# First attention pass on half the array: paired high products for the later query blocks, decay added by VectorE

## Chip, cores and metric

One NeuronCore of a Trainium2 chip runs the whole program as one launch. The metric is the device time of one execution in microseconds (us), as the median of several runs. A smaller number is better.

## What is computed

The reference is one layer of a streaming encoder over 2048 positions of width 1024: a normalisation, one combined projection whose columns are split between eight gated-mixing heads (A) and eight attention heads (B), an output projection, a feed-forward part with a short causal convolution, and a last normalisation, all in float32. The change touches the attention heads alone:

```
def forgetting_attention(q, k, v, f_logit):
    ...
    c = jnp.cumsum(jax.nn.log_sigmoid(f_logit.astype(jnp.float32)), axis=1)
    ...
        s = jnp.einsum('bhtd,bshd->bhts', qi, k, preferred_element_type=jnp.float32) * scale
        s = s + ci[..., :, None] - c[:, :, None, :]
        ...
        s = jnp.where(kpos[None, :] <= qpos[:, None], s, -jnp.inf)
        p = jax.nn.softmax(s, axis=-1)
        return jnp.einsum('bhts,bshd->bthd', p.astype(v.dtype), v)
```

Every score gets a decay, `c[t] - c[s]`, where `c` is a running sum per head. A number that is the same for all keys of one query drops out in the softmax.

## The kernel before

**Precision by parts.** TensorE's operands are kept as a rounded high part and the low remainder. A product of two matrices is then three matmuls (high by high, high by low, low by high), which add up in one PSUM bank. `mm3` does this for the projections: lines 207, 209 and 211, each with 128 rows of contraction and 512 moving columns.

**Stages.** Stage A projects the input (`a_half`). Stage C is the output projection (`c_half`). Stage D is the first half of the feed-forward part (`d_half`, `d_up`). After them come the second half of the tokens and the down projection. The attention is a generator, `b_stream`, that runs as a fill beside these stages: after every projection matmul `tick` counts, and after every 3.5 to 4.4 ticks (`RATES`) it takes one step of the generator. The pieces come in the order query block 0 to 3 (`tb`, 512 queries each) and in it head 0 to 7.

**A piece of attention.** `b_max` is the first pass over a head and a query block: for every key block `sb` of 512 keys up to the diagonal and every chunk `tt` of 128 queries it makes the scores, their least value (scores carry the opposite sign) and a sum of exponentials. `b_mix` is the second pass, which makes the scores again the other way round (lines 774 and 775), exponentiates, and multiplies by the values (lines 762 and 763).

**A chunk of the first pass.** The queries lie in DRAM as `qx` (rows 0 to 63 high, 64 to 127 low), the keys as `kx` (rows 0 to 63 low, 64 to 127 high, 128 and 129 ones, 130 and 131 the decay of the keys in two parts). `cc` holds the decay of the queries. Line 713 multiplies tile `t1` (high queries, `cc`, ones) by tile `m1` (high keys, ones, key decay), so that the decay comes out of the same matmul as the high product: 96 rows of contraction. Line 714 multiplies `t2` by `m2`, both with 128 rows, which gives the two mixed products. Both lines write one PSUM tile of 512 columns, which is called `s` or `dn`: `scores` hands out three tiles `s` and, from stage D on (`self.more`), two tiles `dn` in turn. Off the diagonal VectorE reduces it to its minimum (line 717); on the diagonal it adds the mask and reduces in one instruction (line 719). ScalarE then exponentiates in place (line 722), which frees the tile.

**Decay.** `a_forget` runs four times, once per block of 512 tokens. It transposes a small tile of 16 rows (line 565), makes the running sum `c` (lines 592 to 595), splits it into two parts and writes them to `cc` and to `kx` (lines 597 to 603).

**What sets the order.** The code emits instructions with priorities (the fill and the weight preparation run ahead of their place), and a scheduler with a model of the machine then lays down one fixed order for every engine; on the chip each engine works through its own list in that order. All loads and most stores stand in SyncE's queue (line 99); GpSimd issues the stores of lines 895 and 937 and rounds the weights (line 149). PE in the profile is TensorE, PEld its loading of stationary operands, DVE is VectorE, ACT ScalarE, POOL GpSimd and SP SyncE.

Of the kernel before, what the change touches and what calls it, by code (L numbers as in the profile page):

```python
# [18 lines left out]
P = 128  # L19
# [6 lines left out]
TB = 512  # L26
# [12 lines left out]
BUFS = {  # L39
    "raw": 2, "rawl": 3, "whi": 5, "wlo": 5, "thi": 2, "tlo": 2, "acc": 4,  # L40
# [11 lines left out]
def f32(ap):  # L52
    return ap.bitcast(F32)
# [26 lines left out]
class Block:  # L80
# [134 lines left out]
    def constants(self):  # L215
        nc, a, tc = self.nc, self.a, self.tc
        cp = self.cpool = self.ctx.enter_context(tc.tile_pool(name="const", bufs=1))
        self.ident = cp.tile([P, P], F32, name="ident")
        make_identity(nc, self.ident)
        self.mhalf = cp.tile([P, 8], F32, name="mhalf")  # L220
        nc.gpsimd.memset(self.mhalf, -0.5)
        self.colA = cp.tile([P, 112], F32, name="colA")
        self.colB = cp.tile([P, 88], F32, name="colB")
        self.halo = cp.tile([P, 2 * NF, 2], F32, name="halo")
        nc.gpsimd.memset(self.halo, 0.0)
        dp = self.ctx.enter_context(tc.tile_pool(name="dram", bufs=1, space=DRAM))
        self.ones_d = dp.tile([2, HALF], F32, name="ones_d")
        t = lambda n, k, s: [dp.tile(s, F32, name=f"{n}{i}") for i in range(k)]
        self.qx = t("qx", 2, [8, 128, HALF])
        self.kx = t("kx", 2, [8, 132, HALF])  # L230
        self.cc = t("cc", 2, [8, 2, HALF])
        self.vd = t("vd", 2, [HALF, 8, P])
        self.mixh = t("mixh", 4, [D, TB])
        self.mixl = t("mixl", 4, [D, TB])
        self.rows_d = [t(f"rows{i}_", 8, [P, D]) for i in range(2)]
        self.act_d = [t(f"act{i}_", NF, [P, HALF]) for i in range(2)]
        self.tw_d = t("tw", NF // 2, [P, 2, D])
# [311 lines left out]
    def a_forget(self, half, b):  # L549

        nc, sp, pp = self.nc, self.sp, self.ap
        hT = self.hT[b]
        pl = self.til(pp, [16, TB], F32, "mm")
        for k in range(KC):
            nc.tensor.matmul(pl, lhsT=self.wf[:, k, :], rhs=hT[0][:, k, :], start=k == 0, stop=False)
            self.tick()
            nc.tensor.matmul(pl, lhsT=self.wf[:, k, :], rhs=hT[1][:, k, :], start=False, stop=k == KC - 1)
            self.tick()
        lg = self.til(sp, [16, TB], F32, "ln")
        nc.scalar.activation(lg, pl, AF.Copy)  # L560

        def turn():
            pt = self.til(pp, [P, 4, 16], F32, "tp")
            for i in range(4):
                nc.tensor.transpose(pt[:, i, :], lg[:, i * P:(i + 1) * P], self.ident[:16, :16])
# [12 lines left out]
            nc.vector.tensor_tensor(d, d, ru, op=ALU.mult)  # L578
            nc.scalar.activation(lu, u, AF.Ln)
            nc.vector.tensor_tensor(lu, lu, d, op=ALU.subtract)  # L580
            nc.vector.scalar_tensor_tensor(lu, z, 0.0, lu, op0=ALU.min, op1=ALU.subtract)
            lh = self.til(sp, [P, 4, 8], F32R, "fr")
            ll = self.til(sp, [P, 4, 8], F32R, "fr")
            nc.vector.tensor_copy(lh, lu)
            nc.vector.tensor_tensor(ll, lu, f32(lh), op=ALU.subtract)
            self.defer(70, lambda: cumulate(lh, ll))

        def cumulate(lh, ll):
            pc = self.til(pp, [8, TB], F32, "tp")
            for i in range(4):  # L590
                w, o = self.tri[:, 0:TB - P * i], pc[:, P * i:]
                nc.tensor.matmul(o, lhsT=lh[:, i, :], rhs=w, start=i == 0, stop=False)
                nc.tensor.matmul(o, lhsT=ll[:, i, :], rhs=w, start=False, stop=i == 3)
            c = self.til(sp, [8, TB], F32, "ln")
            nc.vector.tensor_scalar(c, pc, self.carry, None, ALU.add)
            nc.vector.tensor_copy(self.carry, c[:, TB - 1:TB])
            for sc, dst in ((-1.0, self.cc[half]), (1.0, self.kx[half][:, 130:132, :])):
                hl = self.til(sp, [8, 2, TB], F32R, "vn")
                rh, rl = hl[:, 0, :], hl[:, 1, :]
                nc.scalar.activation(rh, c, AF.Copy, scale=sc)  # L600
                nc.vector.scalar_tensor_tensor(rl, c, sc, f32(rh), op0=ALU.mult, op1=ALU.subtract)
# [78 lines left out]
    def b_keys(self, h, sb, values):  # L680
# [9 lines left out]
        self.dma(f32(v), self.vd[hf][sl, h, :].rearrange("(c p) d -> p c d", p=P))  # L690
        return m1, m2, v

    def b_max(self, h, tb):

        nc, bp, pp = self.nc, self.bp, self.bpp
        hf, sl = tb // 2, slice((tb % 2) * TB, (tb % 2 + 1) * TB)
        self.T1.append(self.T1.pop(0))
        t1 = self.T1[0]
        t2 = self.til(self.mp, [P, TB], F32R, "t2")
        self.dma(f32(t1[0:64, :]), self.qx[hf][h, 0:64, sl])  # L700
        self.dma(f32(t1[64:66, :]), self.cc[hf][h, :, sl])
        self.dma(f32(t2), self.qx[hf][h, :, sl])
        nm = self.til(bp, [P, 4, 4], F32, "part")
        ls = self.til(bp, [P, 4, 4], F32, "ls")
        if h % 2 == 0:
            self.rr = self.til(bp, [P, 4, 2], F32, "rr")
        for sb in range(tb + 1):
            m1, m2 = self.b_keys(h, sb, False)
            for tt in range(4):
                ts = slice(tt * P, (tt + 1) * P)  # L710
                n = TB if sb < tb else (tt + 1) * P
                ps = self.scores([P, TB])
                nc.tensor.matmul(ps[:, :n], lhsT=t1[0:96, ts], rhs=m1[0:96, :n], start=True, stop=False)  # L713
                nc.tensor.matmul(ps[:, :n], lhsT=t2[:, ts], rhs=m2[:, :n], start=False, stop=True)  # L714
                dst = nm[:, tt, sb:sb + 1]
                if sb < tb:
                    nc.vector.tensor_reduce(dst, ps, axis=AX.X, op=ALU.min)  # L717
                else:
                    nc.vector.tensor_tensor_reduce(ps[:, :n], ps[:, :n], self.mask[:, 384 - tt * P:], 1.0, 3.0e38,
                                                   ALU.add, ALU.min, dst)  # L720

                nc.scalar.activation(ps[:, :n], ps[:, :n], AF.Exp, scale=-1.0, bias=dst, accum_out=ls[:, tt, sb:sb + 1])  # L722
                yield
        mx = self.til(bp, [P, 4], F32, "mx")
        if tb:
# [3 lines left out]
        m8 = self.til(bp, [P, 4, 2], F32R, "m8")  # L729
# [3 lines left out]
        if tb:  # L733
            k = slice(0, tb + 1)
# [732 lines left out]
```

## Time and profile before

| | |
|---|---|
| median of three runs | 2483.25 us (2481.99 to 2483.38) |
| the profiled execution's own time | 2483.0 us |
| its span, first to last instruction | 2481.3 us |
| mean granted TensorE clock | 0.995 of full speed |
| busy: PE, DVE, ACT, POOL | 98%, 70%, 55%, 14% of the span |

The page gives busy time per engine, the span in 40 slices, the DMA queues, the chain of work that ended last, and the costliest groups of instructions. A group's row reads: line, engine, operation, tile written <- tiles read, shapes, count | busy us, mean ns of one | idle us of the engine before them and what ended most of it. In the timeline a row is: start, duration, engine, line, operation. A matmul's duration there holds its way through the array, and the next one starts before it ends, so what a matmul costs is the step from one start to the next. Shapes are partitions x columns; `16*128` means that 16 rows are contracted and the stationary operand has 128 columns.

### The profile page before, as it was taken

Reading aid. Unit: us, or ns where it says so; the run is one execution under the profiler, and the core shown is the slowest. Engines: PE = TensorE matmul, PEld = TensorE weight load, DVE = VectorE, ACT = ScalarE, POOL = GpSimd, SP = SyncE. Lnnn points to the kernel's source line nnn. Section 1 sums busy time; section 2 is a strip of 40 time slices with the busy share of each in tenths; the row PEclk is TensorE's granted clock in tenths of the full one; section 3 lists DMA queues with packets and bytes.
Section 4 is the critical chain, followed back from the end, with each engine's and each line's share of the span. In section 5 each row is a group of like instructions: output and inputs, shape, how many; then the busy total and the mean of one; then the engine's idle time right before and its main releaser. Section 6 shows DMA issues by size and latency. Waiting matters only on the chain.

```text
span 2481.3 us, 33045 instructions
## 1 busy us (share of the span) xinstructions
PE 2430.5 (98%) x11082; PEld 1995.2 (80%) x11082; DVE 1742.9 (70%) x3116; ACT 1367.4 (55%) x2651; POOL 335.6 (14%) x343
## 2 busy tenths in 40 slices
PE   7998999999999999999999999999999999999998
PEld 5786878878788888888888888878888887888887
DVE  6237677655456878878787775488888887957776
ACT  4327778554355556766677673265555555444443
POOL 3214233010014111211111110100000000001000
PEclk9999999999999999999999999999999999999999
DMA  6863544766867545555555455412222228538633
GB/s 205 239 155 89 155 144 127 189 157 186 284 186 244 156 149 169 176 169 163 175 161 159 154 176 202 144 60 86 92 77 77 93 78 310 169 98 286 210 117 122
DMA packets 346246, 396.35 MB, mean 160 GB/s; under 512 B 52924, under 2 KB 222084, under 8 KB 344652
## 3 DMA queue, kind: packets, MB, share of 16 engines
q1 hardware_dynamic: 341036, 370.11, 48.8%
q0 software_dynamic: 5040, 24.12, 2.5%
q8 instruction: 88, 1.44, 0.2%
q14 instruction: 82, 0.67, 0.1%
HBM read 300.56 MB, written 93.72 MB: 159 GB/s over the span
## 4 chain that ended last, share of the span: by engine, by line
PE 81%; DVE 3%; ACT 2%; DMA 2%; issue 1%; POOL 1%; SPq 0%; DVEq 0%; POOLq 0%; ACTq 0%
PE D L1323 16%; PE mm L209 11%; PE mm L207 11%; PE mm L211 11%; PE A L1120 3%; PE A L1122 3%; PE A L1121 3%; PE o L763 2%; PE o L762 2%; PE s L714 2%; PE s L774 2%; PE s L775 2%; PE s L713 2%; PE B L1121 2%; PE B L1122 2%; PE B L1120 2%
## 5 line engine op out<-in xcount | busy, mean ns | idle before, releaser
L207 PE MATMUL mm<-thi,whi 128*128 128x512 f32 x960 | 378.4, 394 | 0.7 <-DVE vn L417 0.7
L209 PE MATMUL mm<-tlo,whi 128*128 128x512 f32 x960 | 377.5, 393 | 0.0
L211 PE MATMUL mm<-thi,wlo 128*128 128x512 f32 x960 | 377.1, 393 | 0.2 <-DVE wlo L161 0.2
L207 PE MATMUL mm<-whi,thi 128*128 128x512 f32 x640 | 254.4, 399 | 1.8 <-ACT ln L525 1.0
L209 PE MATMUL mm<-wlo,thi 128*128 128x512 f32 x640 | 253.5, 396 | 0.3 <-DVE wlo L161 0.2
L149 POOL TENSOR_SCALAR whi<-raw 128x1024 fp32r<-128x1024 f32 x108 | 127.0, 1176 | 935.6 <-PE mm L209 581.5
L211 PE MATMUL mm<-whi,tlo 128*128 128x512 f32 x640 | 253.3, 396 | 0.0
L722 ACT ACTIVATE s<-s,part 128x512 f32<-128x512 f32 (+3 forms) x257 | 150.7, 587 | 116.7 <-DVE part L717 60.3
L207 PEld LDWEIGHTS mm<-thi,whi 128*128 128x128 f32 x960 | 180.9, 188 | 39.1 <-DVE vn L417 1.1
L211 PEld LDWEIGHTS mm<-thi,wlo 128*128 128x128 f32 x960 | 180.9, 188 | 37.9 <-DVE wlo L161 0.7
L209 PEld LDWEIGHTS mm<-tlo,whi 128*128 128x128 f32 x960 | 180.9, 188 | 37.6
L786 DVE TENSOR_TENSOR pl<-e,ph 128x512 fp32r<-128x512 f32 (+2 forms) x212 | 131.7, 629 | 63.4 <-PE o L763 34.6
L161 DVE TENSOR_TENSOR wlo<-raw,whi 128x1024 fp32r<-128x1024 f32 x108 | 138.2, 1280 | 51.2 <-POOL whi L149 49.7
L780 ACT ACTIVATE e<-s 128x512 f32<-128x512 f32 (+2 forms) x227 | 116.5, 528 | 80.3 <-DVE s L778 38.3
L785 ACT ACTIVATE ph<-e 128x512 fp32r<-128x512 f32 (+2 forms) x212 | 117.4, 562 | 47.5 <-PE o L762 36.7
L207 PEld LDWEIGHTS mm<-whi,thi 128*128 128x128 f32 x640 | 121.7, 190 | 26.5 <-ACT u L507 1.6
L1323 PE MATMUL D<-wl,xh 128*128 128x512 f32 x368 | 141.3, 389 | 0.0
L209 PEld LDWEIGHTS mm<-wlo,thi 128*128 128x128 f32 x640 | 121.7, 190 | 24.3 <-DVE wlo L161 1.0
L1323 PE MATMUL D<-wh,xh 128*128 128x512 f32 x368 | 140.8, 389 | 0.2 <-DVE xo L1401 0.2
L211 PEld LDWEIGHTS mm<-whi,tlo 128*128 128x128 f32 x640 | 121.7, 190 | 24.0
L1323 PE MATMUL D<-wh,xl 128*128 128x512 f32 x368 | 137.2, 389 | 0.0
L717 DVE TENSOR_REDUCE part<-s 128x1 f32<-128x512 f32 x144 | 94.9, 683 | 29.0 <-PE s L714 28.9
(1883 smaller groups left out, 5837.6 us busy)
## 6 DMA issues: line engine op xcount, KB each, us to landing
raw<-in_w_up_dram SPq DMA_DIRECT2D x72, 512.0 KB
m<-kx SPq DMA_DIRECT2D x133, 256.0 KB
m<-kx SPq DMA_DIRECT2D x160, 136.0 KB
x<-act SPq DMA_DIRECT2D x84, 256.0 KB
raw<-in_w_in_dram SPq DMA_DIRECT2D x40, 512.0 KB
v<-vd SPq DMA_DIRECT2D x66, 256.0 KB
x<-in_x_dram SPq DMA_DIRECT2D x24, 512.0 KB
raw<-in_w_out_dram SPq DMA_DIRECT2D x24, 512.0 KB
```

What stands on the lines that cost most here:

```text
L149: self.cast_ins = self.nc.gpsimd.tensor_scalar(out, in_, 1.0, 0.0, ALU.mult, ALU.add).ins
L161: nc.vector.tensor_tensor(lo, raw, f32(hi), op=ALU.subtract)
L207: mm(ps, lhsT=ah[k], rhs=bh[k], start=k == 0, stop=False)
L209: mm(ps, lhsT=ah[k], rhs=bl[k], start=False, stop=False)
L211: self.last_mm = mm(ps, lhsT=al[k], rhs=bh[k], start=False, stop=k == n - 1).ins
L722: nc.scalar.activation(ps[:, :n], ps[:, :n], AF.Exp, scale=-1.0, bias=dst, accum_out=ls[:, tt, sb:sb + 1])
L785: nc.scalar.activation(ph[:, c], e[:, c], AF.Copy)
L786: nc.vector.tensor_tensor(pl[:, c], e[:, c], f32(ph[:, c]), op=ALU.subtract)
L1120: mm(ps, lhsT=xh[:, ks], rhs=yh[:, k, :], start=fresh and k == 0, stop=False, **kw)
L1121: mm(ps, lhsT=xh[:, ks], rhs=yl[:, k, :], start=False, stop=False, **kw)
L1122: mm(ps, lhsT=xl[:, ks], rhs=yh[:, k, :], start=False, stop=k == 3, **kw)
L1323: nc.tensor.matmul(bank[t], lhsT=x[i][:, ts], rhs=w[k], start=fresh and j == 0 and i + k == 0, stop=last and i == 1, **kw)
```

## The change

For query blocks 2 and 3, from the point in stage D at which the two extra score tiles exist, the off-diagonal chunks of the first pass are taken two by two:

- The mixed products (before line 714, now line 748) stay as they are, one matmul of 128 rows for each chunk, and now come first.
- The high products of the two chunks (before line 713, two matmuls of 96 rows) become two matmuls of 64 rows: line 754 uses the upper half of the array (rows 0 to 63, from `t1` and `m1`), line 755 the lower half (rows 64 to 127, from a second copy of the high queries, `tq`, and the high keys that lie in rows 64 to 127 of `m2`). They write different PSUM tiles.
- The decay of the keys is no longer in these matmuls. It is loaded as a tile `cb`, one row of DRAM spread over 128 partitions, and VectorE adds it in the instruction that takes the minimum (`tensor_tensor_reduce`, line 715, as on the diagonal); the exponential follows as before. Both chunks' minima are emitted after the second high product.
- The decay of a query is now the value in the middle of its block, the same for all its 512 queries. `a_forget` writes that to `cc`, keeps `c` of blocks 0 to 2 in DRAM (`cf`), and makes for blocks 2 and 3 the rows `cs` of earlier blocks' `c` less that middle value: two and three loads, subtractions and stores.
- The buffers `tq2` (one) and `cb` (two) are new, and the scratch memory for GpSimd's DMA descriptors shrinks from 8192 to 2048 bytes.

Heads 6 and 7 of block 2 and all heads of block 3 take the new way: 28 pairs of head and key block, 112 chunks, 56 pairs of chunks.

```diff
-    "m1": 2, ... "part": 2, "mx": 2, "m8": 2,
+    "m1": 2, ... "part": 2, "tq2": 1, "cb": 2, "mx": 2, "m8": 2,
...
+            g = 2 * half + b
+            mid = c[:, TB // 2:TB // 2 + 1]
+            if g < 3:
+                self.dma(self.cf[g], c)
+            for k in range(g if g > 1 else 0):
+                ck = self.til(sp, [8, TB], F32, "ln")
+                self.dma(ck, self.cf[k])
+                nc.vector.tensor_scalar(ck, ck, mid, None, ALU.subtract)
+                self.dma(self.cs[g][:, k * TB:(k + 1) * TB], ck)
-            for sc, dst in ((-1.0, self.cc[half]), (1.0, self.kx[half][:, 130:132, :])):
+            for sc, c, dst in ((-1.0, mid.broadcast_to([8, TB]), self.cc[half]), (1.0, c, self.kx[half][:, 130:132, :])):
...
+    def b_least(self, ps, add, nm, ls, tt, sb):
+        nc = self.nc
+        dst = nm[:, tt, sb:sb + 1]
+        if add is None:
+            nc.vector.tensor_reduce(dst, ps, axis=AX.X, op=ALU.min)
+        else:
+            nc.vector.tensor_tensor_reduce(ps, ps, add, 1.0, 3.0e38, ALU.add, ALU.min, dst)
+        nc.scalar.activation(ps, ps, AF.Exp, scale=-1.0, bias=dst, accum_out=ls[:, tt, sb:sb + 1])
...
+        pairs = tb > 1 and self.more
+        if pairs:
+            tq = self.til(self.bx, [P, TB], F32R, "tq2")
+            self.dma(f32(tq[64:128, :]), self.qx[hf][h, 0:64, sl])
...
+            if pairs and sb < tb:
+                cb = self.til(self.bx, [P, TB], F32, "cb")
+                self.dma(cb, self.cs[tb][h:h + 1, sb * TB:(sb + 1) * TB].broadcast_to([P, TB]))
...
-                nc.tensor.matmul(ps[:, :n], lhsT=t1[0:96, ts], rhs=m1[0:96, :n], start=True, stop=False)
-                nc.tensor.matmul(ps[:, :n], lhsT=t2[:, ts], rhs=m2[:, :n], start=False, stop=True)
...
+                alone = sb == tb or not pairs
+                if alone:
+                    nc.tensor.matmul(ps[:, :n], lhsT=t1[0:96, ts], rhs=m1[0:96, :n], start=True, stop=False)
+                nc.tensor.matmul(ps[:, :n], lhsT=t2[:, ts], rhs=m2[:, :n], start=not alone, stop=alone)
+                if alone:
+                    self.b_least(ps[:, :n], self.mask[:, 384 - tt * P:] if sb == tb else None, nm, ls, tt, sb)
+                elif tt % 2 == 0:
+                    ps0, ts0 = ps, ts
                 else:
...
+                    nc.tensor.matmul(ps0, lhsT=t1[0:64, ts0], rhs=m1[0:64, :], start=False, stop=True, tile_position=(0, 0))
+                    nc.tensor.matmul(ps, lhsT=tq[64:128, ts], rhs=m2[64:128, :], start=False, stop=True, tile_position=(64, 0))
+                    self.b_least(ps0, cb, nm, ls, tt - 1, sb)
+                    self.b_least(ps, cb, nm, ls, tt, sb)
...
-    nc = _bacc.Bacc("TRN2", target_bir_lowering=False, num_devices=1, dynamic_dma_scratch_size=8192)
+    nc = _bacc.Bacc("TRN2", target_bir_lowering=False, num_devices=1, dynamic_dma_scratch_size=2048)
```

The code emits the two high products one behind the other, but the scheduler decides where they stand in TensorE's list. These are two places in it. A row is: line, operation, PSUM tile written <- moving tile, stationary tile, shape of the output; the first number behind a name tells buffers of one kind apart.

TensorE before, first key block of head 6 of query block 2, among the value products (`o`, lines 762 and 763) of the piece ahead:

```order
L713 MATMUL dn_2063_8801<-m1_84_538,t1_87_541 128x512
L713 MATMUL s_2062_8793<-m1_84_538,t1_87_541 128x512
L763 MATMUL o_1984_8520<-pl+_2036_8687,v+_2032_8676 128x512
L762 MATMUL o_1984_8520<-ph+_2042_8711,v+_2032_8676 128x384
L763 MATMUL o_1984_8520<-pl+_2043_8712,v+_2032_8676 128x384
L762 MATMUL o_1984_8520<-ph_2046_8727,v+_2032_8676 128x256
L714 MATMUL dn_2063_8801<-m2_2061_8790,t2_2057_8783 128x512
L713 MATMUL dn_2064_8810<-m1_84_538,t1_87_541 128x512
L714 MATMUL s_2062_8793<-m2_2061_8790,t2_2057_8783 128x512
```

TensorE after, the same place (the value products are now lines 797 and 798):

```order
L748 MATMUL dn_2070_8830<-m2_2067_8820,t2_2062_8811 128x512
L755 MATMUL dn_2070_8830<-m2_2067_8820,tq2_2063_8815 128x512
L748 MATMUL dn_2071_8842<-m2_2067_8820,t2_2062_8811 128x512
L798 MATMUL o_1989_8548<-pl_2052_8756,v+_2037_8704 128x256
L797 MATMUL o_1989_8548<-ph_2055_8770,v+_2037_8704 128x128
L748 MATMUL s_2069_8825<-m2_2067_8820,t2_2062_8811 128x512
L754 MATMUL s_2069_8825<-m1_84_543,t1_87_546 128x512
L798 MATMUL o_1989_8548<-pl_2056_8771,v+_2037_8704 128x128
L748 MATMUL s_2072_8847<-m2_2067_8820,t2_2062_8811 128x512
L754 MATMUL dn_2071_8842<-m1_84_543,t1_87_546 128x512
L755 MATMUL s_2072_8847<-m2_2067_8820,tq2_2063_8815 128x512
```

Of the first pair, line 755 now stands in front and its partner, line 754 on tile `s_2069`, five rows further down; between them are four matmuls of 128 rows. The second pair (`dn_2071` and `s_2072`) stands together, in the last two rows.

TensorE before, the second key block of the same piece, between projection matmuls of stage D (lines 207, 209, 211):

```order
L713 MATMUL dn_2069_8847<-m1_85_539,t1_87_541 128x512
L714 MATMUL dn_2069_8847<-m2_2066_8827,t2_2057_8783 128x512
L207 MATMUL mm_2400_10234<-thi_1596_6961,whi_2387_10160 128x512
L209 MATMUL mm_2400_10234<-tlo_1598_6963,whi_2387_10160 128x512
L211 MATMUL mm_2400_10234<-thi_1596_6961,wlo_2388_10161 128x512
L713 MATMUL s_2068_8839<-m1_85_539,t1_87_541 128x512
L714 MATMUL s_2068_8839<-m2_2066_8827,t2_2057_8783 128x512
```

TensorE after, the same place:

```order
L748 MATMUL dn_2077_8881<-m2_2073_8859,t2_2062_8811 128x512
L754 MATMUL dn_2077_8881<-m1_85_544,t1_87_546 128x512
L209 MATMUL mm_2419_10290<-tlo_1603_6991,whi_2405_10211 128x512
L211 MATMUL mm_2419_10290<-thi_1601_6989,wlo_2406_10212 128x512
L207 MATMUL mm_2450_10401<-thi_1777_7704,whi_2402_10205 128x512
L748 MATMUL s_2076_8870<-m2_2073_8859,t2_2062_8811 128x512
L755 MATMUL s_2076_8870<-m2_2073_8859,tq2_2063_8815 128x512
L209 MATMUL mm_2450_10401<-tlo_1779_7706,whi_2402_10205 128x512
```

Here each half-height matmul follows its own chunk's mixed product and has a matmul of 128 rows on both sides. Over the whole list the 112 half-height matmuls make 97 separate stretches: 15 stretches of two (line 754 and then line 755, with nothing between) and 82 of one. All other stretches of TensorE's list hold the same matmuls as before, some of them at another place.

More of the change, by code (lines that the diff above doesn't have):

```diff
@@ L231, in constants @@
         self.cc = t("cc", 2, [8, 2, HALF])
+        self.cf = t("cf", 3, [8, TB])
+        self.cs = [None, None] + [dp.tile([8, g * TB], F32, name=f"cs{g}") for g in range(2, 4)]
         self.vd = t("vd", 2, [HALF, 8, P])
@@ L712, in b_max @@
                 ps = self.scores([P, TB])
[L713 to L717, printed above, removed]
-                else:
-                    nc.vector.tensor_tensor_reduce(ps[:, :n], ps[:, :n], self.mask[:, 384 - tt * P:], 1.0, 3.0e38,
-                                                   ALU.add, ALU.min, dst)
-                nc.scalar.activation(ps[:, :n], ps[:, :n], AF.Exp, scale=-1.0, bias=dst, accum_out=ls[:, tt, sb:sb + 1])
+                alone = sb == tb or not pairs
[6 more added lines that the diff above has]
+                    ps0, ts0 = ps, ts
+                else:
+                    nc.tensor.matmul(ps0, lhsT=t1[0:64, ts0], rhs=m1[0:64, :], start=False, stop=True, tile_position=(0, 0))
+                    nc.tensor.matmul(ps, lhsT=tq[64:128, ts], rhs=m2[64:128, :], start=False, stop=True, tile_position=(64, 0))
+                    self.b_least(ps0, cb, nm, ls, tt - 1, sb)
+                    self.b_least(ps, cb, nm, ls, tt, sb)
                 yield
```

2 rows, old and new, of the table BUFS are left out of this document.

## Prediction

> **What bounds the kernel now.** I read the page first: busy time, then the chain of work that ended last.
>
> ```profile
> span 2481.3 us, 33045 instructions
> ...
> PE 2430.5 (98%) x11082; PEld 1995.2 (80%) x11082; DVE 1742.9 (70%) x3116; ACT 1367.4 (55%) x2651; POOL 335.6 (14%) x343
> ...
> PE 81%; DVE 3%; ACT 2%; DMA 2%; issue 1%; POOL 1%; SPq 0%; DVEq 0%; POOLq 0%; ACTq 0%
> ```
>
> TensorE is busy almost throughout and carries four fifths of the chain. That is an average, so I next asked for the stretch in which the chunks that change are worked on (978 to 1440 us, found by their place in TensorE's list), as busy time and as TensorE's waits.
>
> ```profile
> core 0: us, PE busy (x) PEld busy (x) DVE busy (x) ACT busy (x) POOL busy (x), PEclk, DMA share, GB/s
> 978.00:1440.00 462.00, 461.69 (x2092) 380.37 (x2091) 367.69 (x723) 314.17 (x706) 78.45 (x69) 1.00 0.54 167
> ```
>
> ```profile
> PE s L774 <- DMA m<-kx: 0.2, 1, 0.2
> ```
>
> TensorE waits 0.2 us in 462, at full clock. So a microsecond more or less on TensorE here is one in the total, while VectorE idles 94 us, ScalarE 148 and GpSimd 384. What a matmul costs is read from the timeline, from start to start:
>
> ```profile
> 1026.66 0.40 PE L713 MATMUL s<-m,t 96*128 96x512 f32 x1
> 1026.67 0.19 PEld L713 LDWEIGHTS dn<-m,t 96*128 96x128 f32 x1
> 1026.90 0.40 PE L713 MATMUL dn<-m,t 96*128 96x512 f32 x1
> 1026.90 0.19 PEld L714 LDWEIGHTS s<-m,t 128*128 128x128 f32 x1
> 1027.13 0.39 PE L714 MATMUL s<-m,t 128*128 128x512 f32 x1
> 1027.37 0.40 PE L714 MATMUL dn<-m,t 128*128 128x512 f32 x1
> ```
>
> A matmul of 512 columns costs one step of 0.23 us. The load of the next stationary operand starts with the running matmul and is over (0.19 us) before the next step, so it costs nothing. 96 rows cost no less than 128.
>
> **The change, part by part.**
>
> *What it is for.* A pair of chunks now takes four steps, 0.92 us. If the two half-height matmuls ran side by side, it would take three, and 56 pairs would save 56 x 0.23 = 12.9 us. The order in the section on the change takes most of that away: only 15 pairs stand together. The other 82 half-height matmuls each stand between matmuls of 128 rows, with no partner to run beside, and each replaces one step by one step. Without any cost of switching, the change is therefore worth 15 x 0.23 = 3.5 us.
>
> *What switching costs.* The trace has no matmul on half the rows. The nearest rows are line 565's transposes, which contract 16 rows, on both sides of which stand matmuls of 128:
>
> ```profile
> 548.92 0.39 PE L763 MATMUL o<-pl,v 128*128 128x512 f32 x1
> 549.24 0.13 PEld L565 LDWEIGHTS tp<-ident,ln 16*128 16x128 f32 x1 [0.35 <-ACT ph L785]
> 549.24 0.23 PE L565 MATMUL tp<-ident,ln 16*128 16x16 f32 x1
> 549.39 0.19 PEld L774 LDWEIGHTS s<-t,m 128*128 128x128 f32 x1
> 549.50 0.19 PEld L775 LDWEIGHTS s<-t,m 128*128 128x128 f32 x1
> 549.73 0.40 PE L775 MATMUL s<-t,m 128*128 128x512 f32 x1
> ```
>
> The load for line 565 does not start with the matmul in front (548.92) but 0.32 us later, 0.09 after that matmul's own step is over. The next load of 128 rows has to wait in turn (549.39), and the one behind it follows 0.11 later (549.50), when line 774's columns really begin. The row names ScalarE as what ended the wait, so I looked for another case, where nothing the profile shows was waited for:
>
> ```profile
> 530.18 0.39 PE L211 MATMUL mm<-thi,wlo 128*128 128x512 f32 x1
> 530.50 0.32 PEld L565 LDWEIGHTS tp<-ident,ln 16*128 16x128 f32 x4 [0.35 <-issue]
> 530.84 0.19 PEld L207 LDWEIGHTS mm<-thi,whi 128*128 128x128 f32 x1
> 530.95 0.19 PEld L209 LDWEIGHTS mm<-tlo,whi 128*128 128x128 f32 x1
> ```
>
> The same 0.32 and 0.11. Is it the small size or the transposing? Line 747 transposes too, and is narrow in columns, not in rows:
>
> ```profile
> 1351.46 0.39 PE L209 MATMUL mm<-tlo,whi 128*128 128x512 f32 x1
> 1351.46 0.08 PEld L747 LDWEIGHTS s<-ident,m 128*8 128x8 f32 x1
> 1351.68 0.27 PE L747 MATMUL s<-ident,m 128*8 128x128 f32 x1
> 1351.68 0.19 PEld L774 LDWEIGHTS s<-t,m 128*128 128x128 f32 x1
> 1351.79 0.19 PEld L775 LDWEIGHTS s<-t,m 128*128 128x128 f32 x1
> 1352.03 0.40 PE L775 MATMUL s<-t,m 128*128 128x512 f32 x1
> ```
>
> Here each load starts with the matmul in front. So what costs is leaving the full height of the array and coming back: the loads no longer hide behind matmuls, and each change of height waits for the array to run empty. The Trainium skill, page "TensorEngine Tiling (Array Packing)", section "Key Properties", says that a change of tiling mode drains TensorE, while tiles of one mode work in parallel. By that rule, too, each of the 97 stretches pays twice; the rows of line 565 agree, line 747's, if a narrow stationary operand counts as such a mode, do not.
>
> *The price of one stretch.* Both cases hold three matmuls: one of 512 columns, a small one, one of 512. The first takes 549.73 - 548.92 = 0.81 us, the undisturbed one 1352.03 - 1351.46 = 0.57, so switching costs 0.24. A half-height product streams 512 columns instead of 16, which adds 0.23 x 496/512 = 0.22 to the first; in the undisturbed case its slot grows from 0.11 (1351.68 to 1351.79) to 0.23, by 0.12. A lone half-height matmul thus costs 0.24 + 0.22 - 0.12 = 0.34 us more than the matmul it replaces. Lower end: only the load behind it stays in the open, 0.11. Upper end: its own load takes the full 0.11 as well, 0.45. I take 0.34, since it is read from the same kind of change.
>
> *A stretch of two.* Its second matmul's load follows the first by 0.06 (four loads of line 565 in 0.32 us, one lasting 0.13). If the two stream side by side, a stretch costs 0.34 + 0.06 - 0.23 = +0.17 us against the two matmuls it replaces; the ends are 0.11 + 0.06 - 0.23 = -0.06 and, one behind the other, +0.45. No row shows two halves at work; I take +0.17. The Trainium skill, page "TensorE: Matmul & The Clock Gate", section "Part 3: Packing small matmuls — row/col tiling", gives about 4 ns between the starts of matmuls on different rows. By that figure the 15 stretches would cost +0.11 each instead, 0.9 us less in the sum; no row here shows it.
>
> *VectorE.* The plain minimum of 112 chunks becomes the form with an addend.
>
> ```profile
> L717 DVE TENSOR_REDUCE part<-s 128x1 f32<-128x512 f32 x144 | 94.9, 683 | 29.0 <-PE s L714 28.9
> ...
> L719 DVE CUSTOM_DVE_ANT_0 s<-s,mask 128x512 f32<-128x512 f32 x26 | 18.3, 703 | 6.8 <-PE s L714 5.9 <-ACT s L722 0.8
> L719 DVE DVE_READ_ACCUMULATOR2_ANT part<- 128x1 f32 x128 | 18.0, 141 | 0.0
> ```
>
> That is 703 + 141 - 683 = 161 ns more each, 18.0 us in all; the addend is float32 now, the mask half as wide, and no row shows that. VectorE's 94 idle us hide it, and I take 0. Were the cover gone, a score tile would stay occupied longer and TensorE would wait for one: up to the 18 us.
>
> *Loads and queues.* 28 `cb` of 256 KB and 10 `tq` of 128 KB are 8.4 MB, a tenth of the 77 MB (167 GB/s) that the stretch moves at 0.54 of the DMA engines' time. In SyncE's queue a `cb` waits until VectorE has left one of its two buffers, and behind it stand the keys' tiles and the raw weights; GpSimd, which rounds these, idles 384 of 462 us. The `a_forget` part adds five small subtractions and thirteen small transfers, in front of stores of keys and queries. The nearest price of a late load is this row of TensorE's waits over the whole span:
>
> ```profile
> PE s L713 <- DMA t<-qx: 2.7, 1, 2.7
> ```
>
> I take 0, with -2.7 (a luckier order) to +2.7. The smaller descriptor memory can at worst make a GpSimd store wait for the one before it to land:
>
> ```profile
> tw<-tw POOLq DMA_DIRECT2D x11, 1024.0 KB, 5.2
> act<-va POOLq DMA_DIRECT2D x22, 512.0 KB, 4.5
> ```
>
> Five us on an engine that idles four fifths of the stretch: 0.
>
> *Sum.* 82 x 0.34 + 15 x 0.17 = 27.9 + 2.6 = 30.5 us. The profiled execution took 2483.0 (its span and 1.7 around it; the median of the runs is 0.25 above), so the forecast is 2513.5. With the low ends it is 82 x 0.11 - 15 x 0.06 = 8.1, less 2.7: 2488.4. With the high ends it is 97 x 0.45 = 43.7, and 2.7: 2529.4.
>
> **The rivals.**
>
> - *Half height switches for nothing* (the other side). Then 16 rows are a case of their own, and a half-height load hides behind the matmul in front as line 747's does. For it: only line 565 shows the switch, and with 16 rows, not 64. Against it: just there, where fewer rows are contracted than in the matmuls around, the loads come late. Price: -3.5 us from the 15 pairs, 2479.5, within 0.2% of before. It decides where a stretch costs less than 0.04 us, the 3.5 us spread over the 97 stretches.
> - *The change does what its words say*: all 56 pairs side by side, 2483.0 - 12.9 = 2470.1. The order speaks against it, since TensorE works through its list as it stands.
> - *A light switch*: the array need not run empty, and only the load behind (0.11) and perhaps the one in front stay open. 97 x 0.11 to 97 x 0.22 less the pairs' 3.5: 7 to 18 us, 2490 to 2501.
> - *VectorE holds the score tiles*: the minima come later, both behind the second high product, and five tiles go round. On top of the switch up to 18.0 us: 2514 to 2531. Against it: 0.2 us of waits in this stretch, and a slower TensorE gives VectorE more time. For it: over the whole span TensorE does wait for such tiles, which line 722 frees:
>
> ```profile
> PE s L774 <- ACT s L722: 7.3, 6, 2.3
> ```
>
>
> **How the numbers follow.** The forecast with its neighbourhood (2503 to 2523) gets 0.62, the light switch 0.13, held score tiles beyond 2523 0.07, half height for nothing 0.13, and the two ways to be faster by over 0.2% 0.05: 0.02 for all pairs, 0.03 for a free switch with a luckier order as well. 0.2%, 5 us, is about what a measurement of this kernel can tell from no change. The range 2489 to 2528 leaves out the free switch, the faster cases and a part of the held tiles, about 0.2 together. Slower is 0.62 + 0.13 + 0.07 = 0.82, same 0.13, faster 0.05.
>
> **What would show it.** In the profile after, the loads of lines 754 and 755 should start about 0.32 us after the matmul in front, not with it, and the next load of 128 rows should again come late; from the matmul in front to the second one behind, a lone half-height matmul should take about 1.03 us, against 0.69 now. In a stretch of two, the second should start about 0.06 us after the first. TensorE's waits for other engines should stay near nothing, and the whole loss lie between 978 and about 1470 us. I am wrong if these loads start with the matmul in front, if the loss lies in waits for score tiles, `cb` or keys, or if the time before 978 us moves by more than 3 us.

## The result and the profile after

| | before | after |
|---|---|---|
| median | 2482.62 us (2481.09 to 2483.38, 4 runs) | 2517.03 us (2516.02 to 2525.1, 4 runs) |
| profiled execution, its span | 2483.0, 2481.3 us | 2525.1, 2523.4 us |

The ratio is 1.0148, 95% interval 1.0129 to 1.0167: the change costs 34.4 us. The profiled execution of after is the slowest of its four; the other three took 2516.0 to 2518.0.

I number TensorE's 11082 matmuls in both traces and call **the lag** the start of one after less the start of the one with the same number before (the two lists differ in places, so it need not be the same product). The lag is 5.7 us at 972 us, 38.5 us at 1482 us (times of before) and 42.3 at the end. So 32.8 us come into being in the stretch in which the half-height matmuls run (985.1 to 1475.3 us in the trace of after), 5.7 ahead of it and 3.8 behind it.

The page of after, span and busy times, and the same 462 us as in the prediction, with the same columns (PE, PEld, DVE, ACT, POOL, clock, DMA share, GB/s):

```profile
span 2523.4 us, 33277 instructions
...
PE 2466.2 (98%) x11082; PEld 1987.0 (79%) x11082; DVE 1752.7 (69%) x3233; ACT 1369.6 (54%) x2651; POOL 337.7 (13%) x343
```

```profile
978.00:1440.00 462.00, 461.95 (x1955) 347.82 (x1954) 351.17 (x788) 299.68 (x671) 76.51 (x66) 1.00 0.56 173
```

TensorE looks as busy as before and at full clock, but it gets through 1955 matmuls where it did 2092. VectorE, ScalarE and GpSimd all have less to do in these 462 us: no other engine has become the bound, and from 978 to 1482 us the profile lists no wait of TensorE at all. Busy time alone hides the loss, since the time in which a matmul waits for its turn counts as busy (below, 0.50 us for line 754 and for line 748 behind it, in place of 0.40). The timeline shows it, here one lone half-height matmul:

```profile
1245.19 0.19 PEld L748 LDWEIGHTS dn<-m,t 128*128 128x128 f32 x1
1245.42 0.40 PE L748 MATMUL dn<-m,t 128*128 128x512 f32 x1
1245.74 0.18 PEld L754 LDWEIGHTS dn<-m,t 64*128 64x128 f32 x1 [0.36 <-issue]
1245.74 0.50 PE L754 MATMUL dn<-m,t 64*128 64x512 f32 x1
1246.17 0.19 PEld L748 LDWEIGHTS dn<-m,t 128*128 128x128 f32 x1 [0.25 <-issue]
1246.17 0.50 PE L748 MATMUL dn<-m,t 128*128 128x512 f32 x1
1246.28 0.19 PEld L209 LDWEIGHTS mm<-tlo,whi 128*128 128x128 f32 x1
1246.51 0.40 PE L209 MATMUL mm<-tlo,whi 128*128 128x512 f32 x1
```

The load of line 754 does not start with the matmul in front (1245.42) but 0.32 later: I call this the way in. The next load of 128 rows comes 0.43 after that (1246.17), where the undisturbed step is 0.23: the way back. Line 209's load follows by 0.11. From the matmul in front (1245.42) to the second behind (1246.51) it is 1.09 us against 0.69. A stretch of two:

```profile
987.37 0.18 PEld L754 LDWEIGHTS dn<-m,t 64*128 64x128 f32 x1 [0.24 <-issue]
987.37 0.50 PE L754 MATMUL dn<-m,t 64*128 64x512 f32 x1
987.37 0.18 PEld L755 LDWEIGHTS s<-m,tq 64*128 64x128 f32 x1
987.38 0.50 PE L755 MATMUL s<-m,tq 64*128 64x512 f32 x1
987.80 0.19 PEld L748 LDWEIGHTS s<-m,t 128*128 128x128 f32 x1 [0.25 <-issue]
```

Both halves stream side by side: the second starts 3 ns behind the first in the unrounded records, and the next load comes 0.43 us after the first, as behind a lone one. From the matmul in front to the second behind, the median over the 70 lone stretches with 512 columns on both sides is 1.09 us. Of the 15 stretches of two, four have two full-height matmuls of 512 columns on either side, and these take 1.08 to 1.09. The other eleven have a matmul of 128 columns or another half-height one beside them or one further on, and so do not price a stretch by itself.

### The profile page after: what moved, and what is told of

It is laid out like the page before. It is cut to its first block, busy times and chain, and to the rows that moved or that the text cites. A ratio compares the mean times of both kernels' runs of the same rounds, so it can differ in the third digit from the quotient of the medians.

```text
span 2523.4 us, 33277 instructions
## 1 busy us (share of the span) xinstructions
PE 2466.2 (98%) x11082; PEld 1987.0 (79%) x11082; DVE 1752.7 (69%) x3233; ACT 1369.6 (54%) x2651; POOL 337.7 (13%) x343
## 4 chain that ended last, share of the span: by engine, by line
PE 81%; DVE 3%; DMA 3%; ACT 2%; issue 1%; POOL 0%; SPq 0%; DVEq 0%; POOLq 0%; ACTq 0%
PE D L1358 14%; PE mm L207 11%; PE mm L211 11%; PE mm L209 11%; PE A L1155 3%; PE A L1157 3%; PE A L1156 3%; PE o L798 2%; PE o L797 2%; PE s L748 2%; PE s L810 2%; PE s L809 2%; PE B L1157 2%; PE B L1156 2%; PE B L1155 2%
## 5 line engine op out<-in xcount | busy, mean ns | idle before, releaser
L211 PEld LDWEIGHTS mm<-thi,wlo 128*128 128x128 f32 x960 | 181.1, 189 | 42.3 <-issue 5.8
L815 ACT ACTIVATE e<-s 128x512 f32<-128x512 f32 (+2 forms) x227 | 115.9, 530 | 78.7 <-PE s L810 35.4
L809 PE MATMUL s<-t,m 128*128 128x512 f32 (+3 forms) x253 | 92.0, 369 | 18.6 <-ACT s L716 8.9
```

The lines of the kernel that those rows point to most:

```text
L211: self.last_mm = mm(ps, lhsT=al[k], rhs=bh[k], start=False, stop=k == n - 1).ins
L809: nc.tensor.matmul(ps[:, c], lhsT=m1[:, ks], rhs=t1[:, c], start=True, stop=False)
```

## Experiments

Theory: what costs is leaving the array's full height and coming back, 0.40 us for a lone stretch (1.09 - 0.69) and 0.17 for one of two (1.09 - 4 x 0.23). Rivals: VectorE's addend and the later minima, the new loads and their queue, the preparation in `a_forget`, the new order of the matmuls. In the diffs, `-` and `+` stand against the kernel after, unless said otherwise. "In the stretch" means by how much the lag grew from 972 to 1482 us; for after that is 32.8 us.

**Half height alone.** Against the kernel before:

```diff
-                nc.tensor.matmul(ps[:, :n], lhsT=t1[0:96, ts], rhs=m1[0:96, :n], start=True, stop=False)
+                k = 64 if tb > 1 and self.more and sb < tb else 96
+                nc.tensor.matmul(ps[:, :n], lhsT=t1[0:k, ts], rhs=m1[0:k, :n], start=True, stop=False)
```

> The kernel before with one part of the change alone: in the same 112 chunks line 713 contracts 64 rows instead of 96, on the upper half of the array. It leaves the decay out of these chunks. No cb, tq, addend or new order of the two products. TensorE's list has 87 lone half-height matmuls, 6 stretches of two, 3 of three, 1 of four. Switching theory: 87 x 0.40 and ten longer stretches at 0.40 or more, 39 us or somewhat more over before, 2515 to 2530. VectorE and score tiles, loads and queues: nothing of theirs is there, 2480 to 2486.

Measured: 2518.02 us (2515.7 to 2520.59), ratio 1.0140, 1.0123 to 1.0156; 36.8 us in the stretch. Here 87 of the 112 stand alone, and there are 6 stretches of two, 3 of three and one of four. One number in the kernel before thus costs what the whole change costs, without a load, an addend or a pair more. TensorE's waits in the stretch:

```profile
PE s L775 <- DMA m<-kx: 0.7, 1, 0.7
PE o L764 <- DVE pl+_2121_9037 L787: 0.3, 1, 0.3
```

**68 rows.** The same line with 68 in place of 64.

> The kernel before with one number changed: line 713 contracts 68 rows in place of 96 in the 112 off-diagonal chunks of the later query blocks (rows 68 to 95 hold nothing that counts, so nothing is left out). It is the counterpart of the kernel with 64 rows, which lost 35 us. Theory A (what costs is leaving the array's full height, and an operand of more than 64 rows still takes it whole): 2480 to 2488, the loads of line 713 start with the matmul in front. Theory B (the cost grows as rows get fewer, whatever the tile): most of the 35 us again, 2505 to 2518.

Measured: 2483.06 us (2479.18 to 2485.3, 11 runs), ratio 1.0002, 0.9993 to 1.0011. Theory A's numbers came. In its timeline the load starts with the matmul in front (1107.90 and 1107.91), and the steps are 0.23 again:

```profile
1107.90 0.39 PE L209 MATMUL mm<-tlo,whi 128*128 128x512 f32 x1
1107.91 0.19 PEld L714 LDWEIGHTS dn<-m,t 68*128 68x128 f32 x1
1108.13 0.40 PE L714 MATMUL dn<-m,t 68*128 68x512 f32 x1
1108.13 0.19 PEld L715 LDWEIGHTS dn<-m2+_2377_10116,t 128*128 128x128 f32 x1
```

So fewer rows as such cost nothing: with 68 the loss is gone, with 64 it is there. It fits that 64 rows are run on half the array and 68 on all of it.

**The preparation alone.** `pairs = False`: the middle decay in `cc`, the rows `cs`, the small descriptor memory, and no pair.

> The changed kernel with neither pairs nor the loads of cb and tq: only a_forget's new part, the middle value in cc and the smaller descriptor memory are left. Switching theory: 2480 to 2487 us, no difference to before. If a_forget, the descriptor memory or the shifted order carried a part of the loss, it would show here: 2490 or more.

Measured: 2484.77 us (2476.08 to 2486.58, 10 runs), ratio 1.0000, 0.9989 to 1.0011; 0.3 us in the stretch. The preparation costs nothing that can be measured.

**Undoing the half height, first attempt.**

```diff
+            nc.gpsimd.memset(f32(tq[0:64, :]), 0.0)
...
-                    nc.tensor.matmul(ps0, lhsT=t1[0:64, ts0], rhs=m1[0:64, :], start=False, stop=True, tile_position=(0, 0))
-                    nc.tensor.matmul(ps, lhsT=tq[64:128, ts], rhs=m2[64:128, :], start=False, stop=True, tile_position=(64, 0))
+                    nc.tensor.matmul(ps0, lhsT=tq[:, ts0], rhs=m2, start=False, stop=True)
+                    nc.tensor.matmul(ps, lhsT=tq[:, ts], rhs=m2, start=False, stop=True)
```

> The changed kernel with one thing undone: both high products of a pair run on the full height of the array (128 rows, the upper 64 of the stationary operand zero), and everything else stays: the mixed products first, the decay added by VectorE, the loads of cb and tq, a_forget, the smaller descriptor memory. Switching theory: no stretch of half height is left, so the whole loss goes, 2480 to 2487 us. VectorE and score tiles: nothing that they depend on has changed, so it stays within 5 us of 2517. Loads and queues: the same, 2512 to 2520.

Measured: 2518.49 us (2513.66 to 2523.95), ratio 1.0145, 1.0125 to 1.0166. By the time alone my theory would have fallen. But TensorE now waits, which after does not:

```profile
PE dn L749 <- DMA t<-qx: 15.8, 4, 6.2
PE s L749 <- DMA t<-qx: 11.6, 5, 4.0
```

27 us of waits for queries, with the zeros written anew for every piece, and a granted clock of 0.97 from 972 to 1482 us, where after shows 1.00. The edit brought a loss of its own, so the run tells nothing about the height.

**Second attempt:** one lasting `tq` tile, its zeros written once by VectorE, the matmuls as in the first.

> e1_full_height mended: the zeros in the upper half of tq are written once, by VectorE, and not again for every piece by GpSimd, whose queue made the tile late there. Both high products of a pair run on the full height, all else is as in the changed kernel. Switching theory: 2480 to 2488 us, and no wait of TensorE for tq. VectorE and score tiles, loads and queues: within 5 us of 2517.

Measured: 2514.27 us (2513.39 to 2524.89), ratio 1.0137, 1.0120 to 1.0154; missed again, with the same waits:

```profile
PE dn L752 <- DMA t<-qx: 14.3, 3, 5.3
PE s L752 <- DMA t<-qx: 11.8, 5, 5.3
```

So the zeros were not what made the queries late. What remained was the one buffer that all high products now read, and the new order of the products. The next attempt does without the buffer.

**Third attempt:** full height without the copy.

```diff
-                nc.vector.tensor_scalar(ck, ck, mid, None, ALU.subtract)
+                nc.vector.tensor_scalar(ck, ck, 0.0, None, ALU.mult)
...
-            tq = self.til(self.bx, [P, TB], F32R, "tq2")
-            self.dma(f32(tq[64:128, :]), self.qx[hf][h, 0:64, sl])
+            tq = t1
...
+                    nc.tensor.matmul(ps0, lhsT=t1[0:96, ts0], rhs=m1[0:96, :], start=False, stop=True)
+                    nc.tensor.matmul(ps, lhsT=tq[0:96, ts], rhs=m1[0:96, :], start=False, stop=True)
```

> The change with its high products at full height, but without the second copy of the high queries, whose late load spoiled both earlier attempts: line 754 and line 755 both multiply t1 by m1 with 96 rows of contraction, as line 713 did before. The decay of the keys then comes out of the matmul again, so the row that is loaded as cb is written as zeros; VectorE still adds it and still makes the minima in twos. All else of the change stays: the mixed products first, cb's 28 loads, the middle decay, the descriptor memory. Theory (the price is the switch of height, 0.40 us per lone stretch): nothing left to pay, 2480 to 2488, and in the stretch from 978 to 1482 us TensorE falls behind before by less than 3 us. Rival (the new order of the matmuls, cb's loads or VectorE's longer minima cost the 33 us, and half height is only where it shows): 2505 to 2518. Rival in between (the late load of the copy was itself a part of what after lost): 2480 to 2488 as well, but then after would show waits for that load, which it does not.

Measured: 2492.38 us (2490.55 to 2498.75, 5 runs), ratio 1.0042, 1.0029 to 1.0054. It fell between the two: 24 us of the 34 are gone, 10 remain, and 7.2 in the stretch. Two waits are most of those:

```profile
PE dn L747 <- DMA t<-qx: 3.2, 1, 3.2
PE dn L753 <- DMA m<-kx: 2.2, 1, 2.2
```

**Four buffers for `cb`.** The third attempt with `"cb": 4`, since SyncE's queue stood behind VectorE's use of `cb`.

> The kernel with full-height high products and no second copy of the queries, with four buffers for cb in place of two, nothing else. With two, SyncE's queue stood 36.5 us (24 times) behind VectorE's last use of a cb between 978 and 1482 us, and TensorE waited 3.2 us for queries and 2.2 us for keys whose loads stand behind it in that queue. Theory (a cb load that waits for its buffer holds up the loads behind it): the queue's waits for VectorE's use of cb nearly gone, no wait of TensorE for keys or queries over 1 us in this stretch, 2481 to 2487. Rival (the waits come from the bytes or from the order of the list): 2489 to 2495, with the same two waits.

Measured: 2490.64 us (2485.95 to 2493.23, 9 runs), ratio 1.0029, 1.0019 to 1.0039. The queue's waits before (third attempt) and now, then TensorE's:

```profile
SPq L99 <- DVE part L715: 36.5, 24, 3.9
```

```profile
SPq L99 <- DVE part L715: 35.1, 23, 3.2
```

```profile
PE dn L747 <- DMA t<-qx: 3.1, 1, 3.1
PE dn L753 <- DMA m<-kx: 2.9, 1, 2.9
```

All the same, and the rival's numbers came. Since the queue's waits stayed as they were, the run shows that more buffers do not remove them; whether they make the later loads late it cannot tell.

**High product first again.** The third attempt (two buffers), with the order inside a chunk turned back; the minima stay in twos. The lines that it shares with the third attempt are left out of the diff.

```diff
-                if alone:
-                    nc.tensor.matmul(ps[:, :n], lhsT=t1[0:96, ts], rhs=m1[0:96, :n], start=True, stop=False)
-                nc.tensor.matmul(ps[:, :n], lhsT=t2[:, ts], rhs=m2[:, :n], start=not alone, stop=alone)
+                nc.tensor.matmul(ps[:, :n], lhsT=t1[0:96, ts], rhs=m1[0:96, :n], start=True, stop=False)
+                nc.tensor.matmul(ps[:, :n], lhsT=t2[:, ts], rhs=m2[:, :n], start=False, stop=True)
...
-                    nc.tensor.matmul(ps0, lhsT=t1[0:64, ts0], rhs=m1[0:64, :], start=False, stop=True, tile_position=(0, 0))
-                    nc.tensor.matmul(ps, lhsT=tq[64:128, ts], rhs=m2[64:128, :], start=False, stop=True, tile_position=(64, 0))
```

> The kernel with full-height high products and no second copy of the queries (cb in two buffers, written as zeros), with one thing turned back: in every chunk the high product, 96 rows, comes first again and the mixed product behind it, as before. cb's loads, the addend on VectorE and the minima in twos stay. In the kernel with the mixed product first TensorE waited twice, 3.2 us for t2 at the head of one piece and 2.2 us for a tile m1 later. Theory (the mixed product needs t2 and m2, which are loaded behind t1 and m1, so its coming first makes TensorE want late loads early): no wait for keys or queries over 1 us between 978 and 1482 us, 2481 to 2487, and TensorE at 1482 us less than 2.5 us further behind before than at 972 us. Rival (cb's loads in the queue make them late, whatever the order): 2488 to 2494, with waits of 3 us or more in this stretch.

Measured: 2483.04 us (2479.41 to 2484.84, 11 runs), ratio 0.9998, 0.9989 to 1.0007. The lag grew by 3.4 us in the stretch of the profiled execution, above the 2.5 expected, with small waits, of which one is just above the 1 us expected at most:

```profile
PE s L805 <- DMA m<-kx: 1.1, 1, 1.1
PE dn L745 <- DMA m<-kx: 1.0, 1, 1.0
PE s L745 <- DMA m<-kx: 0.7, 1, 0.7
```

The median settles it. 28 loads of `cb`, 112 additions on VectorE and the minima in twos cost nothing that can be measured. (The ten loads of `tq` are not in this kernel; for them there is only that after shows no wait for queries.) The 10 us of the third attempt go with the mixed product standing first. Why is shown in part: that product needs `t2`, which is loaded behind `t1`, and this fits the wait of line 747, 3.2 us for queries. The other, 2.2 us, is the high product's (line 753) for its `m1`, and stays unexplained. After has the same order and shows no such wait in the stretch; that its slower TensorE comes for the tiles later would explain that, but was not tested by itself.

**No addend.** The pairs as in after, with the plain minimum (`None` for `cb`).

> The changed kernel with the plain minimum in the paired chunks: the decay is left out of these. cb is still loaded but not read. TensorE's list has 88 stretches of one and 12 of two. Switching theory: 88 x 0.40 + 12 x 0.17 = 37 us over before, 2514 to 2524. VectorE and score tiles: 18 us of VectorE's work are gone, so clearly less than 2517, 2485 to 2505.

Measured: 2530.70 us (2528.47 to 2536.9), ratio 1.0197, 1.0183 to 1.0211: above the range, though VectorE does less. In the stretch it is 36.5 us (88 lone stretches, 12 of two), so the addend was not the cost there. The other 12 us arise between 838 and 884 us, ahead of the stretch; the next run shows the same.

**Loads alone.** `alone = True`: `cb` and `tq` are loaded, and nothing reads them; every chunk is computed as before.

> The changed kernel without the pairs: all chunks take the old way (96 rows with the decay in them, plain minimum), but cb and tq are still loaded, a_forget still makes cf and cs, cc holds the middle value and the descriptor memory is small. Switching theory: 2480 to 2487 us. VectorE and score tiles: also 2480 to 2487, since the addend is gone. Loads and queues: the loss is still there, over 2500.

Measured: 2496.59 us (2491.79 to 2503.17), ratio 1.0058, 1.0037 to 1.0080. The time lies between the two forecasts. In the stretch it is 4.4 us; 11 arise between 838 and 884 us. The window from 830 to 890 us, before and here, and TensorE's waits in it here:

```profile
830.00:890.00 60.00, 58.95 (x265) 48.27 (x264) 49.05 (x85) 32.87 (x71) 19.95 (x17) 1.00 0.58 181
```

```profile
830.00:890.00 60.00, 51.47 (x198) 40.97 (x197) 32.20 (x65) 25.54 (x51) 11.03 (x11) 0.86 0.85 243
```

```profile
PE s L747 <- DMA t<-qx: 3.2, 1, 3.2
PE o L798 <- DVE pl L821: 3.2, 1, 3.2
PE s L809 <- DMA m<-kx: 2.1, 1, 2.1
```

22 of the 28 `cb` loads stand in these 60 us. All 28 are issued between 818 and 889 us here, and between 825 and 1458 in after. As I read it, without a reader their two buffers are free at once, so the loads come long before their place. The DMA share rises from 0.58 to 0.85, TensorE waits 8.5 us, and the granted clock shows 0.86 in place of 1.00. Taking readers away moved the loads, so this run and the one before do not price the loads of after; the kernel with the high product first does it for `cb`, at nothing.

**Pairs kept together.** The two half-height matmuls issued behind the second mixed product and given priority:

```diff
-                nc.tensor.matmul(ps[:, :n], lhsT=t2[:, ts], rhs=m2[:, :n], start=not alone, stop=alone)
+                low = nc.tensor.matmul(ps[:, :n], lhsT=t2[:, ts], rhs=m2[:, :n], start=not alone, stop=alone)
...
+                    with self.tc.issue_after(low.ins), self.tc.high_priority(AHEAD_W):
```

> The changed kernel with the two high products of a pair held back until the second chunk's mixed product is issued and then given a high priority. TensorE's list now has 48 stretches of two and 16 of one, instead of 15 and 82. Switching theory, with the prices from the changed kernel's trace (0.40 us for a stretch of one, 0.17 for a stretch of two): 16 x 0.40 + 48 x 0.17 = 14.6 us over before, 2497, 2491 to 2502. If two halves did not run side by side it would be 64 x 0.40 = 25.6, 2508. VectorE and score tiles: the first chunk's tile is held longer still, so no better than 2517. Were height switched for nothing: 48 x 0.23 = 11 us less than before, 2472.

Measured: 2494.80 us (2494.34 to 2498.29), ratio 1.0052, 1.0037 to 1.0067; 13.7 us in the stretch. Of the half-height matmuls 96 now stand in 48 stretches of two and 16 alone: 48 x 0.17 + 16 x 0.40 = 14.6. The 40 stretches of two with 512 columns on both sides take 1.09 us in the median. The sum of prices holds for another mixture, and even 56 clean pairs would cost 56 x 0.17 = 9.5 us.

**Four at a time.** The same means, with all four mixed products of a key block first and then four half-height matmuls in turn (upper, lower, upper, lower).

> The high products of four chunks held back together: four mixed products, then four half-height ones in turn above and below. TensorE's list has 17 stretches of four, 5 of three, 6 of two, 17 of one. Switching theory with a step of 0.22 us for a second pair in a stretch (its loads hidden): a stretch of four costs 0.40 + 0.22 - 3 x 0.23 = -0.07 us, so the sum is 17 x 0.40 + 6 x 0.17 + 5 x 0.16 - 17 x 0.07 = 7.4 us over before, 2490. With a second pair's step of 0.43 (drain or loads in the open within the mode too): 12 us, 2495. VectorE and score tiles: four of five tiles are held at once, so TensorE waits for them, 2500 or more.

Measured: 2486.79 us (2483.63 to 2495.81, 12 runs), ratio 1.0022, 1.0012 to 1.0031; 7.5 us in the stretch, with 17 stretches of four, 5 of three, 6 of two and 17 alone. One of four:

```profile
1184.83 0.39 PE L748 MATMUL s<-m2+_2538_10750,t 128*128 128x512 f32 x1
1185.15 0.18 PEld L758 LDWEIGHTS dn<-m,t 64*128 64x128 f32 x1 [0.36 <-issue]
...
1185.26 0.19 PEld L758 LDWEIGHTS s<-m,t 64*128 64x128 f32 x1
1185.26 0.19 PEld L760 LDWEIGHTS s<-m2+_2538_10750,tq 64*128 64x128 f32 x1
1185.49 0.39 PE L758 MATMUL s<-m,t 64*128 64x512 f32 x1
1185.49 0.39 PE L760 MATMUL s<-m2+_2538_10750,tq 64*128 64x512 f32 x1
1185.82 0.19 PEld L747 LDWEIGHTS dn<-m,t 96*128 96x128 f32 x1 [0.37 <-issue]
```

Inside the half height the loads hide again (1185.26, while the first pair streams). The way back comes 0.67 us after the first load (1185.15 to 1185.82) in place of 0.43, so the second pair costs 0.24, one undisturbed step for two matmuls. With 512 columns on both sides a stretch of four takes 0.32 + 0.67 + 0.11 + 0.23 = 1.33 us (the one shown has 128 columns behind it; the seven with 512 take 1.32 in the median) against 6 x 0.23 = 1.38 undisturbed: even, at last, and no more.

## Why the prediction was right

The forecast was 2513.5, the median is 3.5 above it. By its own steps:

- *The way in.* Predicted: the load 0.32 us after the matmul in front. Measured: 0.32. The 16-row row of line 565 was the right neighbour for 64 rows.
- *One lone stretch.* Predicted 1.03 us to the second matmul behind, measured 1.09; so +0.40, not +0.34. The mis-sized step is the way back, 0.43 in place of the 0.37 that remain of 1.03 after 0.32, 0.11 and 0.23. On 82 stretches that is 4.9 us, within the upper end of 0.45.
- *A stretch of two.* The second was to start 0.06 us behind the first; it starts at 3 ns. The way back is longer by as much, so the two errors cancel: that +0.17 came out is luck. The Trainium skill's page "TensorE: Matmul & The Clock Gate", section "Part 3: Packing small matmuls — row/col tiling", was the better guide to the start: about 4 ns there, 3 here.
- *The sum.* With measured prices 82 x 0.40 + 15 x 0.17 = 35.4 us; the lag grew by 32.8 in the stretch. Where the 2.6 between them lie was not followed. The forecast's sum was 30.5: the lone stretches priced 4.9 too low are its error, and the measured loss of 34.4 is larger by 3.9.
- *VectorE.* Line 715 with `cb` took what the row with the mask had promised, float32 or not, here with its time per instruction in ns behind the comma:

```profile
L715 DVE CUSTOM_DVE_ANT_0 s<-s,cb 128x512 f32<-128x512 f32 x64 | 43.8, 703 | 7.0 <-PE s L755 4.9 <-PE s L754 1.3 <-ACT dn L716 0.3
```

  The cover was real: taken at 0, and the kernel with all of VectorE's work at full height took 0.9998 of before.
- *Loads, queues, preparation.* Taken at 0; right for the preparation alone and for the loads of `cb` with the high product first. What the prediction did not name is the turned order of the two products, which costs 10 us at full height. That it does not show in after was good fortune, not foreseen.
- *The time before 978 us* was to move by no more than 3 us, and it moved by 5.7. By the prediction's own words that counts against it. The bound was too tight: in the ten other kernels, all but the two whose `cb` loads run ahead, the lag at 972 us lies between -6.15 and +2.4 us, so one profiled execution does not resolve 3 us here. The 5.7 is above all of these, though. The profiled execution is also 8.1 us above the median of its four, and 9.5 of its lag lie outside the stretch. What made them was not traced.
- *The rivals.* Half height for nothing fell with the kernel that has 64 rows and nothing else; the light switch with the 0.40 that a lone stretch costs, where it allowed 0.11 to 0.22; score tiles held by VectorE with the empty list of waits and with the full-height kernel at 2483.04. All pairs side by side was right that pairs overlap, and wrong about the order (15 pairs of 56) and the price: a way in and a way back take more than one overlap gives.

The Trainium skill's page "TensorEngine Tiling (Array Packing)", section "Key Properties", says that a change of tiling mode drains the array. The 64-row and the 68-row kernel agree with it, where rows decide the mode; the price, 0.40 us alone and 0.17 for a pair, is from these runs.

## What to carry to other kernels

Half of the array is worth its use only where several half-height matmuls stand one behind the other: in these kernels each visit has a way in of 0.32 and a way back of 0.43 us in place of steps of 0.23; with 512 columns a pair loses 0.17, and four are even. Read the order that the scheduler made before counting on neighbours, and keep a small contraction above 64 rows (68 cost nothing, nothing between was tried) where it would stand alone among full ones. When an experiment undoes one part, look at the waits before the verdict: two of the undone kernels here lost as much as the change, by waits of their own.

## What the runs showed that I had not expected

- Two matmuls on different halves of the array start 3 ns apart, and the load behind them comes no later than behind a single one (0.43 us); within the half height a second pair costs 0.24 us.
- 68 rows of contraction cost the same as 96 or 128, while 64 among full-height matmuls cost 0.40 us more.
- Loads that nobody reads are not harmless: 22 transfers of 256 KB stood in 60 us, and in that window TensorE waited 8.5 us and the granted clock was 0.86.
- Which of two products comes first in a chunk was worth 10 us at full height (2492.38 against 2483.04); only one of the two waits behind it is explained.
